# A hybrid decoder trunk on one core: side tasks of the first mixer handed out per row tile and held between projection matmuls, the residual's transposes held until the output projection

## The chip, the cores and the metric

The kernel runs on one core of one Trainium2 chip. The time is the device time of one execution in microseconds (us). The kernel before was timed three times on the chip, and once more under the hardware profiler; all numbers of the trace below come from that profiled execution.

## What is computed

A trunk of two residual layers over 256 tokens of width 2048, in float32. Each layer is a mixer, a cross-attention into 256 memory tokens, and a SwiGLU feed-forward block; each of the three normalises its input and adds its result to the residual stream `h`.

```
for layer in range(2):
    hn = rms_norm(h, ln_mix[layer])
    mix = nsa_retention_mixer(hn, ...) if layer == 0 else gated_deltanet_mixer(hn, ...)
    h = h + mix
    h = h + memory_cross_attention(rms_norm(h, ln_mem[layer]), mem, ...)
    h = h + swiglu_ffn(rms_norm(h, ln_ffn[layer]), ...)
```

The first mixer has one input projection. It feeds eight attention heads (a branch over compressed blocks, one over selected blocks, one over a window; at 256 tokens all blocks are selected) and four retention heads. The compressed branch takes overlapping blocks of 32 tokens and sends them through a small two-layer network (`nsa_cmp_w1`, `nsa_cmp_w2`). An output projection joins all heads.

## The kernel before, in words

**Projections.** Activations lie transposed in SBUF, 128 features to a tile. A projection (`Proj`) loops over the 16 row tiles of its weight (44 in the output projection of a feed-forward block). `load_weight` fetches 512 KB by DMA from the queue of SyncE (SP), two row tiles of 512 columns at a time, into four buffers. `split_weight` (L214, L215) splits each piece of 128 x 512 into a high part, rounded to fp32r by ScalarE (ACT), and the low rest, by VectorE (DVE); four buffers hold each. `passes` (L237) then issues three fp32r matmuls per product: high by high, high by low, low by high. In the form "f" (weights stationary) a row tile of 512 columns is four column blocks of three passes, 12 matmuls with 256 moving columns. In the form "t" (activations stationary) it is two token halves of three passes, 6 matmuls with 512 moving columns. The four column blocks write two PSUM tiles, two blocks in each.

**Work beside projections.** Everything else is written as generators, called tasks: they do a piece of work and yield a number. `Proj.step` counts issued work in units of a 256-column matmul; each time 6 units are full, `tick` advances a counter `now` by one and resumes each task that is due. A task that yields n is due 2n counts later, at least 1. A row tile is 12 units, so before the change there are two ticks in a row tile, and `yield 1` is one row tile. `finish(ts)` ticks on the spot, with no projection between, until the given tasks are done. Four PSUM banks serve the tasks; `take(n)` waits for n of them, `give(n)` returns them.

**Order on the engines.** The program is traced in the order above. A scheduler then orders each engine's queue by a timeline of its own: an instruction traced earlier goes first if its data are there by then, and a later one passes it if they are not. `tc.issue_after(i)` adds an order edge: what is traced inside the block on the engine of `i` stands behind `i` in that engine's queue. On the chip each queue runs in its order.

**The first mixer** (`mix0`, L699). `nsa_keys` projects keys and values in three projections of 16 row tiles, then spawns the two tasks `compress`, one for keys and one for values. Two query projections of 16 row tiles follow; behind each, four heads of the generator `head` are spawned. `finish(cmp)` ends the compress tasks. `retention` follows with eight projections of 16 row tiles, in two groups (query, key, value, gate); at the end of each group two tasks `ret_head` are spawned, and those of the first group are finished on the spot. The output projection is `residual` with `early=12`: the first 12 row tiles of two of its four column groups go first.

`compress` (L858 on) loads `nsa_cmp_w1` in 8 loads of 512 KB, each for four steps of k, and yields 1 after every second k: 16 yields, 4 matmuls before each (L882, L883; the shape is 128 x 256). Its tail follows: copy (L887), transposes (L890), sigmoid, second product (L901 or L912), norm, and the copy of the keys to `kcat` (L908).

`head` waits until both compress tasks are done and takes three banks. It issues the scores (L795 to L798) and two transposes for the queries' norm (L386); a chain over ACT and DVE turns them into scaled softmax rows `s` (L801 to L828); `yield 5`; it transposes `s` (L833 to L838) and copies the results to SBUF (`pTc` L839, `px` L842, `py` L843); `yield 2`; it multiplies with the values (L847 to L851), and gives its banks back. `ret_head` issues scores, `yield 2`, products, `yield 3`, transposes (L986).

**The last feed-forward block** (`ffn`, L626 on). 11 pairs of projections (gate and up, form "f") fill the hidden activations; 4 output projections in the form "t" follow, 44 row tiles each. Beside the first of these the task `turn` transposes the residual stream back: 8 groups of 4 transposes (L672), each copied by ACT (L675) with `yield 2` after it.

Of the kernel before, what the change touches and what calls it, by code (L numbers as in the profile page):

```python
# [2 lines left out]

# [1 line left out]

# [13 lines left out]
P = 128  # L19
# [59 lines left out]
def trunk(ctx: ExitStack, tc: tile.TileContext, a: dict, out: bass.AP, phases=ALL):  # L79
# [7 lines left out]
    sp = ctx.enter_context(tc.tile_pool(name="sp", bufs=2))  # L87

    sp.tile([P, 112], F32, name="pad", bufs=1)
    state = {"now": 0, "banks": 4, "wide": None}  # L90
    dp = ctx.enter_context(tc.tile_pool(name="dp", bufs=1, space=DRAM))
    psj = ctx.enter_context(tc.tile_pool(name="psj", bufs=4, space=PSUM))
    psg = ctx.enter_context(tc.tile_pool(name="psg", bufs=4, space=PSUM))
# [18 lines left out]
    def tick():  # L112
        state["now"] += 1
        for t in list(tasks):
            if t.ready <= state["now"]:
                try:
                    t.ready = state["now"] + max(1, int(2 * (next(t.gen) or 1)))
                except StopIteration:
                    t.done = True
                    tasks.remove(t)  # L120
# [97 lines left out]
    def load_weight(W, k0, nk, c0, ncol, g=None):  # L218
# [10 lines left out]
            parts += [(h[:, i, :], l[:, i, :]) for i in range(m)]  # L229
        return parts  # L230

    def passes(o, x, w, start, last, x_stationary=False):

        (xh, xl), (h, l) = x, w
        pairs = ((xh, h), (xh, l), (xl, h)) if x_stationary else ((h, xh), (h, xl), (l, xh))
        for j, (s_, m) in enumerate(pairs):
            PE.matmul(o, s_, m, start=start and j == 0, stop=last and j == 2, skip_group_check=True)  # L237

    class Proj:

# [50 lines left out]

        def step(self, n):
            self.count += n
            while self.count >= 6:
                self.count -= 6
                tick()

    def proj(W, c0, segs, x, KT=KD, g=None):
        return Proj(W, c0, segs, x, KT, g).run()
# [254 lines left out]
    def cross_attention(l, side):  # L554
        with pool("xax", side=side) as xx, pool("xas") as xs, pool("xa", 2) as xp:
            xb = split_x(xx)
            x = fill_x(xb, 1, l)
            kt = xs.tile([P, 4, T], F32, name="kt")
            vt = xs.tile([P, 2, 512], F32, name="vt")
            S.dma_start(kt, kv[l][0])  # L560
# [65 lines left out]
    def ffn(l, last):  # L626
        Wi, Wo = a["ffn_w_in"][l], a["ffn_w_out"][l]
        with pool("ff") as fp, pool("ft", 2) as ft:
            hh = fp.tile([P, KF, T], F32R, name="hh")
            hl = fp.tile([P, KF, T], F32R, name="hl")  # L630
            with pool("ffx", side="right") as fx:
                x = fill_x(split_x(fx), 2, l)
                rb = None
                ns = None
                for b in range(KF // 4):
                    pg = proj(Wi, b * 512, [("f", 512)], x)[0]
                    if rb is None:
                        rb = rstd_bc()
                    gs = []
                    for i in range(2):  # L640
                        g = ft.tile([P, 2, T], F32, tag="fg", name="fg", bufs=3)
                        for j in range(2):
                            V.tensor_mul(g[:, j], pg[i][:, j], rb)
                        ns = S.activation(g, g, AF.Silu)
                        gs.append(g)
                    pu = proj(Wi, FH + b * 512, [("f", 512)], x)[0]
                    for i in range(2):
                        g = gs[i]
                        k = 4 * b + 2 * i
                        u = ft.tile([P, 2, T], F32, tag="fu", name="fu")  # L650
                        for j in range(2):
                            V.tensor_mul(u[:, j], pu[i][:, j], rb)
                        V.tensor_mul(u, u, g)
                        S.activation(hh[:, k : k + 2], u, AF.Copy)
                        V.tensor_sub(hl[:, k : k + 2], u, hh.bitcast(F32)[:, k : k + 2])
                with tc.issue_after(ns.ins):
                    S.preload_act_table_set(LNEXP)
            hx = lambda k: (hh[:, k, :], hl[:, k, :])
            if not last:
                residual(Wo, hx, KF)  # L660
                return
            with pool("ffo", side="right") as fo:

                xt = fo.tile([P, 2, D], F32, name="xt")

                def turn():
                    for b in range(4):
                        for t in range(2):
                            yield from take(1)
                            p = bank()  # L670
                            for f in range(4):
                                PE.transpose(  # L672
                                    p[:, f * P : (f + 1) * P], xT[:, b * 4 + f, t * P : (t + 1) * P], ident
                                )
                            S.activation(xt[:, t, b * 512 : (b + 1) * 512], p, AF.Copy)  # L675
                            give(1)
                            yield 2

                spawn(turn())
                for b in range(4):  # L680
                    po = proj(Wo, b * 512, [("t", 512)], hx, KF)[0]
                    for t in range(2):
                        o = xt[:, t, b * 512 : (b + 1) * 512]
                        V.tensor_add(o, o, po[t])
                        S.dma_start(out[0, t * P : (t + 1) * P, b * 512 : (b + 1) * 512], o)
# [13 lines left out]
    def mix0(xb, close):  # L699
        W = a["hyb_w_in"][0]  # L700
        done = {}
        with pool("m0o") as op:
            oh = op.tile([P, 16, T], F32R, name="moh")
            ol = op.tile([P, 16, T], F32R, name="mol")
            cm = op.tile([P, 512 + 4 * 384 + 1], F32, name="cmix")
            S.dma_start(cm, a["c_mix"])
            with pool("ns") as np_:
                x = parts(xb)
                ck = pool("cmpk", side="right")
                with pool("wide", 2) as state["wide"]:  # L710
                    nsa, cmp = nsa_keys(W, x, np_, ck.__enter__(), cm)
                with pool("nt", 2) as nt:
                    for blk in range(2):
                        pq = proj(W, blk * 512, [("f", 512)], x)[0]
                        for i in range(4):
                            h = blk * 4 + i
                            q = nt.tile([P, T], F32, tag="q", name="q", bufs=8)
                            S.activation(q, pq[i // 2][:, i % 2, :], AF.Copy)
                            done[h] = spawn(nsa(nt, h, q, oh, ol))
                    finish(cmp)  # L720
                    ck.__exit__(None, None, None)
                    with pool("rt", 2) as rt_:
                        retention(W, x, rt_, oh, ol, cm, done)

                        def mo(k):
                            finish([done[k]])
                            return oh[:, k, :], ol[:, k, :]

                        residual(a["hyb_w_out"][0], mo, 16, early=12)
                        drain()  # L730
            close()
# [263 lines left out]

    def mix1():
        W = a["gdn_w_in"][0]
        with pool("gr") as r_:


# [533 lines left out]
```

## Time and profile before

| | us |
|---|---|
| median of 3 runs | 3003.91 |
| lowest, highest | 3001.68, 3008.66 |
| the profiled execution, its own time | 3001.64 |
| its span, first to last instruction | 2999.8 |
| TensorE (PE) busy in the span | 2957.6 |
| VectorE (DVE) busy | 2033.3 |
| ScalarE (ACT) busy | 1703.5 |

The mean granted TensorE clock is 0.997 of its upper level, 2.4 GHz. Matmuls overlap in the array, so a matmul's own duration (about 280 ns for 256 columns) is longer than the time from its start to the next one's. The pace of a stream is therefore its time divided by its matmuls. A float32 matmul of the tasks that is not a transpose stands in the trace as two records.

### The profile page before, as it was taken

To read this page: it belongs to the slowest core of one execution; us is meant where nothing else is said; L and a number is where in the kernel's file an instruction comes from. 1 tells how busy PE (TensorE), PEld (TensorE's weight loads), DVE (VectorE), ACT (ScalarE), POOL (GpSimd) and SP (SyncE) were. 2 spreads that over 40 slices of the span, in tenths; PEclk is the share of its full clock that TensorE was granted. 3 is DMA by queue.
4 is the path that set the end of the run, shared out by engine and by line. 5 is a ranking of instruction groups with operands and counts; after the bars stand their busy time and mean duration, and the time that the engine had idled before them with its cause. 6 is when DMAs were issued, how large, how long until landed. Compare 5 with 4: busy or idle time off the path is not lost.

```text
span 2999.8 us, 59557 instructions
## 1 busy us (share of the span) xinstructions
PE 2957.6 (99%) x22917; PEld 2830.7 (94%) x22917; DVE 2033.3 (68%) x3879; ACT 1703.5 (57%) x3328; POOL 110.3 (4%) x153
## 2 busy tenths in 40 slices
PE   8999999999999999999999989999999999999999
PEld 8989899999999999999978989999999999999887
DVE  6867676776665665557689978886667656655554
ACT  6655655665555554447665657776556555445444
POOL 0000000000000000000110101121000000000000
PEclk9999999999999999999999999999999999999999
DMA  7776555656666665566677676663656666666665
GB/s 237 203 233 178 156 147 176 186 174 195 193 195 193 195 195 193 196 191 187 185 220 230 178 208 178 176 177 127 194 187 182 191 193 194 184 189 183 197 199 166
DMA packets 327641, 566.97 MB, mean 189 GB/s; under 512 B 41868, under 2 KB 71620, under 8 KB 327100
## 3 DMA queue, kind: packets, MB, share of 16 engines
q1 hardware_dynamic: 321280, 545.02, 61.0%
q10 hardware_dynamic: 3500, 10.33, 1.3%
q0 software_dynamic: 2576, 7.82, 0.9%
q8 instruction: 179, 2.93, 0.4%
q14 instruction: 106, 0.87, 0.1%
HBM read 549.16 MB, written 13.93 MB: 188 GB/s over the span
## 4 chain that ended last, share of the span: by engine, by line
PE 94%; DMA 2%; DVE 2%; ACT 1%; issue 1%; POOL 0%; SPq 0%; ACTq 0%; DVEq 0%; POOLq 0%
PE pj L237 87%; DVE w_lo L215 1%; DMA w<-in_hyb_w_in 1%; DMA d_T<-AB 1%; PE slv L1458 0%; PE slv L1455 0%; PE slv L1444 0%; ACT w_hi L214 0%; DMA w<-in_nsa_cmp_w 0%; DVE xT L424 0%; POOL AB L1350 0%; DVE x_lo L357 0%; DMA mraw<-in_mem 0%; PE slv L1452 0%; PE qk L1071 0%
## 5 line engine op out<-in xcount | busy, mean ns | idle before, releaser
L215 DVE TENSOR_TENSOR w_lo<-w,w_hi 128x512 fp32r<-128x512 f32 x1938 | 1328.0, 691 | 829.9 <-ACT w_hi L214 818.2
L214 ACT ACTIVATE w_hi<-w 128x512 fp32r<-128x512 f32 x1938 | 1215.1, 631 | 1127.5 <-DVE w_lo L215 591.8
L237 PE MATMUL pj<-x_hi,w_hi 128*128 128x256 f32 (+1 forms) x4496 | 1248.4, 280 | 16.0 <-ACT w_hi L214 15.7
L237 PE MATMUL pj<-x_lo,w_hi 128*128 128x256 f32 x4496 | 1244.0, 279 | 0.0
L237 PE MATMUL pj<-x_hi,w_lo 128*128 128x256 f32 (+1 forms) x4496 | 1225.2, 280 | 0.9 <-DVE w_lo L215 0.9
L237 PEld LDWEIGHTS pj<-x_hi,w_hi 128*128 128x128 f32 (+1 forms) x4496 | 848.4, 189 | 19.5 <-ACT w_hi L214 17.4
L237 PEld LDWEIGHTS pj<-x_lo,w_hi 128*128 128x128 f32 x4496 | 845.6, 188 | 0.8
L237 PEld LDWEIGHTS pj<-x_hi,w_lo 128*128 128x128 f32 (+1 forms) x4496 | 831.6, 188 | 3.2 <-DVE w_lo L215 2.3
L237 PE MATMUL pj<-hl,w_hi 128*128 128x256 f32 x704 | 193.7, 276 | 0.0
L237 PE MATMUL pj<-hh,w_hi 128*128 128x256 f32 x704 | 193.6, 276 | 0.0
L237 PE MATMUL pj<-hh,w_lo 128*128 128x256 f32 x704 | 192.4, 276 | 0.0
L237 PE MATMUL pj<-o,w_hi 128*128 128x256 f32 x1024 | 182.4, 281 | 1.3 <-ACT o L1013 1.1
L237 PE MATMUL pj<-w_lo,x_hi 128*128 128x512 f32 (+2 forms) x448 | 172.0, 385 | 2.6 <-DVE w_lo L215 2.3
L237 PE MATMUL pj<-w_hi,x_lo 128*128 128x512 f32 (+2 forms) x448 | 168.0, 376 | 0.0
L237 PEld LDWEIGHTS pj<-o,w_hi 128*128 128x128 f32 x1024 | 155.9, 189 | 2.0 <-ACT o L1013 1.3
L237 PE MATMUL pj<-o,w_lo 128*128 128x256 f32 x512 | 141.6, 281 | 0.0
L237 PE MATMUL pj<-w_hi,x_hi 128*128 128x512 f32 (+2 forms) x448 | 140.5, 380 | 0.5 <-ACT w_hi L214 0.4
L237 PE MATMUL pj<-w_hi,hl 128*128 128x512 f32 x352 | 138.3, 393 | 0.0
L237 PE MATMUL pj<-w_lo,hh 128*128 128x512 f32 x352 | 137.7, 391 | 0.0
L237 PEld LDWEIGHTS pj<-hh,w_hi 128*128 128x128 f32 x704 | 132.1, 188 | 0.0
L237 PEld LDWEIGHTS pj<-hl,w_hi 128*128 128x128 f32 x704 | 132.1, 188 | 0.0
L237 PEld LDWEIGHTS pj<-hh,w_lo 128*128 128x128 f32 x704 | 131.3, 188 | 0.0
(416 smaller groups left out, 3613.1 us busy)
## 6 DMA issues: line engine op xcount, KB each, us to landing
w<-in_ffn_w_in SPq DMA_DIRECT2D x352, 512.0 KB, 4.2
w<-in_gdn_w_in SPq DMA_DIRECT2D x193, 512.0 KB, 4.2
w<-in_ffn_w_out SPq DMA_DIRECT2D x176, 512.0 KB, 3.7
w<-in_hyb_w_in SPq DMA_DIRECT2D x96, 512.0 KB, 3.7
w<-in_gdn_w_out SPq DMA_DIRECT2D x64, 512.0 KB, 4.4
w<-in_xa_wkv SPq DMA_DIRECT2D x32, 512.0 KB, 4.4
w<-in_hyb_w_out SPq DMA_DIRECT2D x32, 512.0 KB, 4.7
w<-in_nsa_cmp_w SPq DMA_DIRECT2D x16, 512.0 KB, 5.0
```

Source lines behind the costliest of these rows:

```text
L214: state["hi"] = S.activation(h, w, AF.Copy)
L215: state["lo"] = V.tensor_sub(l, w, h.bitcast(F32))
L237: PE.matmul(o, s_, m, start=start and j == 0, stop=last and j == 2, skip_group_check=True)
```

## The change

In the first mixer `state["beat"]` is 12 instead of 6, until the cross-attention sets it back. A tick then comes once in a full row tile; `now` still advances by two in it. A task sleeps at least 4 counts, two row tiles. The tick runs inside `together`: all matmuls and transposes that the tasks trace in it stand behind the last projection matmul traced, and the next projection matmul stands behind the last of them in trace order. Ticks of `finish` are not held. In the last feed-forward block the transposes of `turn` stand behind the last projection matmul traced when they are traced; its beat stays 6.

```diff
-    state = {"now": 0, "banks": 4, "wide": None}
+    state = {"beat": 6, "now": 0, "banks": 4, "wide": None}
...
-                    t.ready = state["now"] + max(1, int(2 * (next(t.gen) or 1)))
+                    t.ready = state["now"] + max(4 if state["beat"] > 6 else 1, int(2 * (next(t.gen) or 1)))
...
+    @contextmanager
+    def together():
+
+        traced = nc.cur_bb.bb.instructions
+        n = len(traced)
+        mm = state["mm"].ins
+        with tc.issue_after(mm):
+            yield
+        own = [i for i in traced[n:] if i.engine == mm.engine]
+        if own:
+            state["after"] = own[-1]
+
     def passes(o, x, w, start, last, x_stationary=False):
...
         for j, (s_, m) in enumerate(pairs):
-            PE.matmul(o, s_, m, start=start and j == 0, stop=last and j == 2, skip_group_check=True)
+            after = state.pop("after", None)
+            with tc.issue_after(after) if after is not None else nullcontext():
+                state["mm"] = PE.matmul(o, s_, m, start=start and j == 0, stop=last and j == 2, skip_group_check=True)
...
         def step(self, n):
             self.count += n
-            while self.count >= 6:
-                self.count -= 6
-                tick()
+            while self.count >= state["beat"]:
+                self.count -= state["beat"]
+                state["now"] += state["beat"] // 6 - 1
+                if state["beat"] > 6:
+                    with together():
+                        tick()
+                else:
+                    tick()
...
             x = fill_x(xb, 1, l)
+            state["beat"] = 6
...
-                            for f in range(4):
-                                PE.transpose(
-                                    p[:, f * P : (f + 1) * P], xT[:, b * 4 + f, t * P : (t + 1) * P], ident
-                                )
+                            with tc.issue_after(state["mm"].ins):
+                                for f in range(4):
+                                    PE.transpose(
+                                        p[:, f * P : (f + 1) * P], xT[:, b * 4 + f, t * P : (t + 1) * P], ident
+                                    )
...
     def mix0(xb, close):
         W = a["hyb_w_in"][0]
         done = {}
+        state["beat"] = 12
...
     def mix1():
         W = a["gdn_w_in"][0]
+        state["beat"] = 6
```

## Rows read from the trace of the kernel before

**Rows 1.** The page: busy times of the engines; shares of the chain that ended last.
```profile
PE 2957.6 (99%) x22917; PEld 2830.7 (94%) x22917; DVE 2033.3 (68%) x3879; ACT 1703.5 (57%) x3328; POOL 110.3 (4%) x153
...
PE 94%; DMA 2%; DVE 2%; ACT 1%; issue 1%; POOL 0%; SPq 0%; ACTq 0%; DVEq 0%; POOLq 0%
```

**Rows 2.** Stretches: length, busy PE PEld DVE ACT POOL (x), granted clock, DMA share, GB/s.
```profile
188.00:231.00 43.00, 39.27 (x317) 37.72 (x316) 33.91 (x60) 28.98 (x58) 0.00 (x0) 1.00 0.90 276
231.00:262.60 31.60, 31.49 (x255) 29.64 (x255) 20.57 (x58) 18.55 (x53) 0.00 (x0) 1.00 0.63 188
262.60:371.00 108.40, 108.40 (x703) 97.86 (x701) 78.10 (x224) 62.40 (x166) 0.00 (x0) 1.00 0.54 155
```

**Rows 3.** The chain that ended last, in pieces: start, us, what, matmuls merged.
```profile
269.34 0.43 PE nC L847 x2
...
494.56 88.34 PE pj L237 x750
...
653.36 706.41 PE pj L237 x6188
...
2488.03 0.33 PE g L672 x3
2488.36 43.54 PE pj L237 x384
...
2532.01 224.69 PE pj L237 x1888
```

**Rows 4.** The residual's transposes: all of them, and the one at 2531.74 us.
```profile
L672 PE MATMUL g<-ident,xT x32: 270/272/273, 2312.4 to 2764.6; 128*128 128x128 f32 x32
...
2531.74 0.27 PE L672 MATMUL g<-ident,xT 128*128 128x128 f32 x1
```

**Rows 5.** PE by line, 188 to 262.6 us: count, busy us, mean ns, idle before.
```profile
L237 PE MATMUL pj<-x_hi,w_hi 128*128 128x256 f32 x133 | 36.8, 284 | 0.5 <-ACT w_hi L214 0.5
...
L882 PE MATMUL cmp<-w_hi,cfp 128*128 128x256 f32 x64 | 16.5, 290 | 3.2 <-ACT w_hi L214 3.2
```

**Rows 6.** ACT in order of time: start of the copies behind the second query projection.
```profile
262.62 0.62 ACT L718 ACTIVATE q<-pj 128x256 f32<-128x256 f32 x2
```

**Rows 7.** DMA from 188 to 231 us: packets, and compress's loads.
```profile
DMA packets 9864, 11.88 MB, mean 276 GB/s; under 512 B 366, under 2 KB 7805, under 8 KB 9860
...
w<-in_nsa_cmp_w SPq DMA_DIRECT2D x14, 512.0 KB, 5.0
```

**Rows 8.** One head in order of time on PE and DVE: start us, us, engine, line.
```profile
272.28 0.38 PE L386 MATMUL nC<-ident,q 128*128 128x128 f32 x2
...
282.81 0.75 DVE L828 TENSOR_SCALAR s<-s,st 128x16 f32<-128x16 f32 x3
...
283.96 0.27 PE L838 MATMUL nB<-ident,s 128*7 128x128 f32 x1
...
292.66 0.39 PE L851 MATMUL nC<-py,vw 128*128 128x128 f32 x2
...
293.32 0.38 PE L386 MATMUL nC<-ident,q 128*128 128x128 f32 x2
```

**Rows 9.** The tail of compress in order of time: its first and its last instruction.
```profile
233.42 0.37 ACT L887 ACTIVATE chs<-cmp 60x256 f32<-60x256 f32 x1
...
249.21 0.24 DVE L908 COPY kcat<-kn 128x15 f32<-128x15 f32 x2
```

**Rows 10.** Busy time by stretch, columns as in rows 2: two standstills of PE.
```profile
149.50:153.00 3.50, 0.67 (x6) 0.46 (x4) 0.33 (x1) 0.99 (x2) 0.00 (x0) 1.00 0.97 278
...
1780.00:1782.00 2.00, 0.00 (x0) 0.00 (x0) 0.00 (x0) 0.00 (x0) 0.00 (x0) 1.00 0.64 157
...
1784.00:1786.00 2.00, 0.00 (x0) 0.00 (x0) 0.00 (x0) 1.29 (x6) 1.26 (x2) 0.50 1.01 388
```

**Rows 11.** PE in order of time: the output projection's first matmul, the retention heads' last transposes.
```profile
482.18 0.28 PE L237 MATMUL pj<-moh,w_hi 128*128 128x256 f32 x1
...
494.18 0.38 PE L986 MATMUL rs<-ident,ry 128*128 128x128 f32 x2
```

More of the change, by code (lines that the diff above doesn't have):

```diff
@@ L1 @@
 import math
-from contextlib import ExitStack
+from contextlib import ExitStack, contextmanager, nullcontext
 import numpy as np
```

## The prediction

> **What bounds the kernel now.** I read the page first: TensorE is busy for 99% of the span and holds 94% of the chain that ended last, the vector engine is at 68% [rows 1]. So a change pays only where the matmul queue stands still or runs below its best pace, and it costs where it makes that queue wait. The change touches two stages: the first mixer (from about 114 to 583 us) and the last feed-forward block (2267 to 2998 us). I then read the stages by stretches [rows 2]: in the mixer PE has idle time in one stretch only, 188 to 231 us, where the two compress tasks load their weights beside the first query projection and DMA runs at 276 GB/s; from 262.6 us on PE is busy without a break. "Busy" hides the pace, so the third view is the chain in pieces, as time per matmul [rows 3]. A piece of 384 projection matmuls takes 43.54 us, 113.4 ns each, and the 6188 of the first feed-forward block 114.2 ns (a few wide ones among them). But 750 in a row from 494.56 us, most of them the first mixer's output projection, take 88.34 us, 117.8 ns each, with nothing between them. There are two paces, 4.4 ns apart, and a stream keeps the one that it has until something else is put into it. The last feed-forward block shows the moment of a fall: at 2531.74 us one hoisted transpose of the residual stands between two passes of one product, and the 1888 matmuls behind it take 224.69 us, where the five like pieces before it ran at 113.4 ns [rows 3, 4].
>
> **The transposes of the last block.** All 32 transposes of `turn` are traced beside the output projection, yet run from 2312.4 us on [rows 4], up to 440 us early, at several places three together. Three cost 0.33 us on the chain and will cost it at their new place, so 32 are 3.5 us before and after. What goes is the slow pace behind the last hoisted one: 1888 x (117.8 - 113.4) ns = 8.3 us. By the piece itself it would be 224.69 - 1888 x 0.1134 = 10.6 us, but its end holds the first wider matmuls of the output projection, so 10.6 is the upper end. The lower end is zero, if some other event sets the slow pace. I take 8.3: after the change nothing is left to interrupt that stream, and the same stream in the first block kept the fast pace for 706.41 us [rows 3]. The output stage needs the transposed residual only when a whole projection of 44 row tiles is done (about 60 us), so eight groups, two row tiles apart, are hidden there; no DMA and no queue but PE, and ACT's eight copies behind it, sees them move.
>
> **The first mixer: compress.** A row tile is 12 matmuls, 1.36 us. Work beside it was handed out twice per row tile; it is now handed out once, and a task sleeps at least two row tiles. The compress loop, 16 steps of one row tile each, so stretches from 16 to 32 row tiles, the whole of both query projections. Its 16 loads of 512 KB leave SP's queue in the order of the handing out, so they are spread too, between the projections' 16. Now: from 188.0 us to the copies of the second query block at 262.62 [rows 6], 74.6 us pass. PE issued in them some 400 projection matmuls (three groups of about 133, one of them shown) and 2 x 64 of compress [rows 5], 528 x 0.1134 = 59.9 us; of the 572 matmuls in all [rows 2] 44 are others, 5.9 us at an estimated 0.13, a little over a transpose's 0.11: 65.8 us. So 8.8 us are lost, 3.7 of them as idle time before 231 us [rows 2]. After: 32 loads are 16.8 MB, 61 us at the 276 GB/s that DMA gave [rows 7], less than PE's 66. PE sets the time, with little to spare. Gain between 0 (DMA no better placed) and 8.8; I take 7, as most of the demand that overran DMA is moved to where DMA now runs at 188 GB/s [rows 2].
>
> **The first mixer: the hold.** Each tick's matmuls now stand behind the last projection matmul traced, and the first pass of the next row tile stands behind the last of them. If one waits for its data, that pass waits too, and with it everything that accumulates into its bank. What may go on are the other three column blocks of the next rows, as far as four split weights reach: 4 rows x 9 passes = 36 matmuls, 4.1 us. Today the scheduler simply lets a late task slide: the head that I followed has its scores at 272.28 us, its scaled scores finished at 283.56, its first transpose at 283.96 and its output at 292.66 [rows 8], and the next head's scores end 21 us after its own, though the yields ask for 7 row tiles.
> The first head is held worst. Compress now ends at row tile 31 of 32, so its tail (copy, transposes, sigmoid, second product, norm) runs after the second query projection, and the head's scores behind that. The transposes are due five row tiles later. Data: tail 16.1 us now, 233.42 to 249.45 [rows 9], of which its bare instructions are some 8.5; scores 1.8; scores to scaled scores 272.66 to 283.56, 10.9 [rows 8]; together 21 to 29 us. PE has six row tiles (8.2), tail and scores (3.3) and the 4.1 that may run ahead: 15.6. PE stands for 5 to 13 us. Elsewhere a standstill from 1780 us on brought the granted clock from 1.00 to 0.50 by 1784, while one inside 149.5 to 153 us left it at 1.00 [rows 10]; some 6 us of work at half clock would cost 3 us more. I take 6: the tail is long now because its matmuls stand behind projection matmuls that will be used up.
> The seven other heads come every 8 row tiles: PE has 8 x 1.36 + 4.4 for the head = 15.3 us of work (a 256-wide float32 product is 0.43 [rows 3], the others in proportion: scores 1.8, transposes 0.9, output 1.7); a head's own cycle is 1.8 + 10.9 + last transposes and copies 1.2 + output 1.7 + 0.5 to the next = 16.1. So 0.8 us each, 5.6 us; between 0 and 7 x (10.9 - 5 x 1.36) = 29, if nothing may run ahead. I take 4, as the vector engine is freer of split weights while PE waits. The retention heads of group 0 are handed out without a hold. Those of group 1 are held at the start of the output projection; now their last transposes come 12 us after its first matmul, 482.18 to 494.18 [rows 11], and the hold gives them six row tiles (8.2), their own products (5) and the 4.1: nothing.
> Last, the output projection behind the mixer, and the first of the next stage, run at the slow pace now: 750 x 4.4 ns = 3.3 us. Which pace it has after the change depends on the last held group; I count half, 1.6.
>
> **Sum.** -8.3 - 7 + 6 + 4 - 1.6 = -6.9 us against the profiled execution's own 3001.6 us (span 2999.8): 2994.7. The median of the runs shown, 3003.9, is 2.3 us above that execution, so 2997.0. A change under 0.2%, 6 us, can hardly be told from none here.
>
> **Rivals.**
> (a) The mixer gains all it can: the holds cost nothing because their data are there, compress gives 8.8 and the output projection is fast. -8.3 - 8.8 - 3.3 = -20.4: 2983.5. For it: PE is the only full engine. Against it: the cycle of 16.1 against 15.3.
> (b) The pace is not what the transpose set, or the transposes in the output stage only trade one slow stretch for another; the mixer is even. Then the time is that of before, 3004. Against it: five pieces of 384 before 2531 us and the whole first block are fast. The Trainium skill, "TensorE: Matmul & The Clock Gate", section "Back-to-back issue gap", gives one gap for a width, N/2.4 + 2.5 ns, an estimated 109 ns here, and knows no second pace. By that rule the holds buy nothing; the two rows at 113.4 and 117.8 with clock and width the same speak against it. An equal result comes if the mixer costs 8 where I have 1.4.
> (c) Slower: the hold turns the heads' latency into PE time. Place: the transposes of each head, 5 row tiles behind its scores. If nothing runs ahead of a held pass, each waits 10.9 - 6.8 = 4.1 us, 7 x 4.1 = 29 us, and the first head 9 more: -8.3 - 7 + 29 + 9 - 1.6 = +21: 3025. It decides from about 1.6 us per head on, where the sum turns positive. For it: a head takes 21 us now and is asked for in 15.3; the rotary work of two projections stands in the vector engine's queue as well. Against it: the scheduler reorders passes of different column blocks already.
>
> **Chances.** Forecast (2991 to 3000) 0.46, (a) 0.14, (b) and an even sum 0.20, (c) in any size above +6 us 0.20. The forecast's larger part, below 2998, and (a) with its near cases make faster 0.48; (b) and the rest of the forecast same 0.31; slower 0.21. For 8 in 10 the range reaches to (a)'s end, 2984, and to half of (c), 3014.
>
> **What will show it.** Right: no transposes of the residual before 2750 us, and the gate and up projections at 113.4 ns to their end; compress over some 60 us without DMA waits; the heads every 15 to 17 us. Wrong: PE idle before a head's transposes in more than the first head, a granted clock below 1.00 in the mixer, or a stretch of 117.8 ns in the last block all the same.

## The result, and the profile after

The changed kernel takes 3024.13 us (median of 4 runs, 3021.59 to 3026.58), the kernel before 3002.8 in the runs beside it: a ratio of 1.0065, 95% interval 1.0053 to 1.0077. It is slower by some 0.65%; the forecast of 2997 and its range up to 3014 are both missed. The profiled execution took 3021.59 us, its span is 3019.8 against 2999.8.

The page of the changed kernel, busy times and shares of the chain that ended last:

```profile
PE 2961.8 (98%) x22917; PEld 2827.4 (94%) x22917; DVE 2038.7 (68%) x3879; ACT 1709.8 (57%) x3328; POOL 111.5 (4%) x153
...
PE 92%; DVE 3%; DMA 2%; ACT 1%; issue 1%; POOL 0%; ACTq 0%; SPq 0%; DVEq 0%; POOLq 0%
```

Against [rows 1] the instructions are as many, PE is busy 4.2 us longer and the span is 20 us longer. Most of the time was not worked, it was waited.

To find where, the mixer is cut at copies that both kernels make. A begins at the copy of the last key and value projection and ends at the copies of the second query projection (compress runs here). B goes on to the first gate copy of retention group 0, four projections later (the heads run here). C ends at the first value copy of group 1. The stretches A, B and C of the changed kernel (length; busy PE, PEld, DVE, ACT, POOL; granted clock; DMA share, GB/s):

```profile
191.03:258.00 66.97, 65.91 (x509) 61.66 (x510) 46.25 (x77) 42.12 (x80) 0.00 (x0) 1.00 0.81 243
258.00:409.33 151.33, 133.88 (x805) 115.76 (x804) 100.75 (x328) 78.92 (x243) 0.00 (x0) 0.95 0.40 113
...
409.33:485.57 76.24, 76.20 (x534) 71.04 (x533) 52.41 (x106) 39.31 (x73) 0.00 (x0) 1.00 0.59 170
```

The same stretches A, B and C of the kernel before:

```profile
190.08:262.62 72.54, 68.70 (x554) 65.31 (x553) 52.49 (x114) 46.02 (x107) 0.00 (x0) 1.00 0.79 241
262.62:370.38 107.76, 107.76 (x698) 97.29 (x697) 77.48 (x221) 61.78 (x166) 0.00 (x0) 1.00 0.55 156
370.38:457.32 86.94, 86.94 (x608) 80.54 (x607) 65.52 (x177) 48.87 (x123) 0.00 (x0) 1.00 0.51 146
```

There B and C have no idle time, at a clock of 1.00. B has grown by 43.6 us, and stands idle for 151.33 - 133.88 = 17.5 of them; C is 10.7 shorter, since heads that slid into C before are done in B. A is 5.6 shorter. With 0.9 us lost ahead of A, 2.6 less in the gate projection behind C, 2.7 more in the output projection, which now has the retention heads' rest in it, and 1.1 less in the stage after it, the mixer is 27.2 us behind. Another 1.2 us is lost on the way to the last block, and there 8.4 are won: 20.0.

PE's waits from 258 to 410 us (waiting tile, for whom: us in all, times, longest):

```profile
PE nB L860 <- DVE s L850: 10.3, 4, 6.3
PE nA L855 <- DVE s L850: 6.2, 7, 1.3
PE nA L818 <- DVE kcat L930: 0.8, 1, 0.8
```

L855 and L860 are the heads' transposes, `s` their scaled scores: 16.5 of the 17.5 us are PE standing in front of a transpose whose data are not there. One head, in order of time (in brackets the wait ahead of an instruction):

```profile
305.84 0.38 PE L405 MATMUL nC<-ident,q 128*128 128x128 f32 x2
...
318.32 0.62 DVE L850 TENSOR_SCALAR s<-s,st 128x7 f32<-128x7 f32 x3
...
318.61 0.28 PE L860 MATMUL nB<-ident,s 128*7 128x128 f32 x1 [1.83 <-DVE s L850]
...
319.60 0.75 DVE L850 TENSOR_SCALAR s<-s,st 128x16 f32<-128x16 f32 x3
...
320.14 0.33 PE L855 MATMUL nA<-ident,s 128*128 128x128 f32 x1 [0.82 <-DVE s L850]
```

Compare [rows 8]. Between the last scores and the first transposes of the seven later heads the trace has 72 to 84 projection matmuls (counted as 256 wide), where the kernel before let some 92 to 97 pass in most heads; the first head has none there. The chain over DVE and ACT is not shorter for that: here 305.84 to 320.35 us. PE stands twice, because the scores of the second token half are ready 1.4 us after those of the first. And the standstills have a second price. Three short stretches behind them (columns as above):

```profile
280.00:287.00 7.00, 5.59 (x24) 4.95 (x25) 3.51 (x14) 3.46 (x10) 0.00 (x0) 0.54 0.00 0
...
316.00:324.00 8.00, 5.35 (x29) 4.62 (x28) 4.08 (x17) 4.36 (x16) 0.00 (x0) 0.79 0.17 60
...
357.00:361.50 4.50, 3.68 (x13) 2.88 (x13) 1.66 (x7) 1.61 (x3) 0.00 (x0) 0.62 0.00 0
```

The clock fell from its upper level to the lower one. Up to 7 x 0.46 + 8 x 0.21 + 4.5 x 0.38 = 6.6 us of work are lost so, beside the idle time; a part of it falls into idle time and is counted twice.

What the forecast had right stands in the pieces of the chain, and in the transposes of the residual by line:

```profile
525.47 85.37 PE pj L251 x753
...
2313.25 457.66 PE pj L251 x4035
2770.91 0.44 PE g L693 x4
...
L693 PE MATMUL g<-ident,xT x32: 271/272/273, 2770.8 to 2793.7; 128*128 128x128 f32 x32
```

The gate and up projections run in one piece at 113.4 ns a matmul, and the transposes wait until the output projection [rows 3, 4]. The first mixer's output projection is at 113.4 ns too, where it was at 117.8.

### The profile page after: what moved, and what is told of

It reads as the page before. It is cut to its first block, busy times and chain, and to the rows that moved or that the text cites. A ratio compares the mean times of both kernels' runs of the same rounds, so it can differ in the third digit from the quotient of the medians.

```text
span 3019.8 us, 59529 instructions
## 1 busy us (share of the span) xinstructions
PE 2961.8 (98%) x22917; PEld 2827.4 (94%) x22917; DVE 2038.7 (68%) x3879; ACT 1709.8 (57%) x3328; POOL 111.5 (4%) x153
## 4 chain that ended last, share of the span: by engine, by line
PE 92%; DVE 3%; DMA 2%; ACT 1%; issue 1%; POOL 0%; ACTq 0%; SPq 0%; DVEq 0%; POOLq 0%
PE pj L251 85%; DVE w_lo L215 1%; DMA d_T<-AB 1%; ACT w_hi L214 0%; PE slv L1481 0%; PE slv L1478 0%; DMA w<-in_hyb_w_in 0%; PE slv L1467 0%; DVE xT L443 0%; PE cmp L905 0%; ACT s L846 0%; POOL AB L1373 0%; DVE x_lo L376 0%; DMA mraw<-in_mem 0%; PE slv L1475 0%
```

## The experiments

Theory H: the hold itself costs, as PE waits for the heads' chain. Theory B: the rarer and later handing out costs. In the expectations a stage's loss is its length less its matmuls at the fast pace (113.2 ns for a projection's of 256 columns, about 2 ns and 0.83 ns a column for one record of a float32 one). Lengths and losses, in us, with the ratio to before and its interval; worked out from the time lines of the profiled runs (one execution each):

```
                           A           B           C       ratio
before                  72.5  9.7  107.8  1.6   86.9  1.4  1
changed kernel          67.0  9.0  151.3 30.9   76.2  2.1  1.0065 [1.0053, 1.0077]
e1  transposes only     73.0 10.8  107.8  1.6   86.9  1.4  0.9972 [0.9962, 0.9982]
e2  no hold             59.8  2.6  109.8  2.7  102.1 12.7  0.9980 [0.9970, 0.9990]
e3  heads free          67.9  9.9  107.8  3.0  106.2 16.4  1.0020 [1.0012, 1.0029]
e4  only heads held     59.4  2.2  145.2 24.8   77.5  1.3  1.0019 [1.0008, 1.0029]
e5  e4, sleep 7         60.7  3.5  129.5 14.0   82.9  1.8  0.9986 [0.9977, 0.9995]
e6  all held, sleep 7   67.2  9.3  133.8 16.9   79.7  2.0  1.0033 [1.0024, 1.0043]
e7  edge in front only  67.6 10.3  107.8  3.0  107.2 17.4  1.0035 [1.0022, 1.0048]
e9  e5, first head 11   59.7  2.0  121.7 11.8   89.0  2.1  0.9978 [0.9968, 0.9988]
e10 e5, first head free 60.5  3.3  130.6 15.0   83.0  1.8  1.0001 [0.9992, 1.0010]
e11 edge behind only    60.6  2.8  149.9 29.9   79.0  2.3  1.0050 [1.0037, 1.0063]
e13 e1, compress 24     64.1  6.2  109.4  1.2   96.3  8.8  0.9978 [0.9967, 0.9988]
e14 e1, compress 20     70.4 10.3  109.2  1.3   92.8  6.5  0.9979 [0.9970, 0.9989]
```

Two things have to be kept in mind with these rows. Runs with the same mixer as e1 (e8, e12, e15 to e18; e17 differs only behind C) have an A of 71.1 to 74.0 us, so 1 or 2 us in A are nothing; their B and C agree to 0.1. And the output projection behind C, which no column holds, ran at the fast pace in the changed kernel, e3 to e7, e9 to e11, e13 and e14, and at the slow pace in the kernel before, e1 and e2: 3 us.

**e1: the last block's transposes alone.**

```diff
     def mix0(xb, close):
...
-        state["beat"] = 12
+        state["beat"] = 6
```

> The mixer stays as before (two ticks in a row tile, no hold); only the 32 transposes of the last block are held until the output projection. Both theories on the mixer expect the same here: all 4035 matmuls of the last gate and up stream at 113.4 ns, 8.3 us less than before, about 2994.5. If that stream's pace hung on something else in the changed kernel, a stretch of 117.8 ns stays in the last block and the time is 3003.

Measured 0.9972, 8.4 us of 3005.7. The piece of the chain:

```profile
2289.19 457.67 PE pj L251 x4035
```

As expected to 0.1 us. The same kernel on another chip (e18) gave 0.9970.

**e2: no hold in the mixer.**

```diff
-                if state["beat"] > 6:
-                    with together():
-                        tick()
-                else:
-                    tick()
+                tick()
```

> The changed kernel without the hold in the mixer: one tick in a row tile, sleeps of at least two row tiles, but the tasks' matmuls may slide. Theory H (the hold makes PE wait for the heads' vector and scalar chain): the heads' idle time before their transposes and the falls of the granted clock go, 25 to 30 us less than the changed kernel, 2992 to 2998. Theory B (handing out late is the fault: compress ends behind the second query projection, the heads start late and bunched): at most 8 us less than the changed kernel, above 3015, with the idle time between 258 and 410 us still over 8 us.

Measured 0.998, 2998.1 us: H's side. But the table shows something that neither theory had. A loses 2.6 us instead of 10.8: the stretched compress does save what the forecast claimed. B is even. C loses 12.7. PE's long wait there, and the two ends of the heads' stretch (the keys' copy that lets the first head begin; the first scores of a retention head, which here wait for `mol`, the last instruction of an attention head):

```profile
PE nB L856 <- DVE s L846: 5.2, 1, 5.2
```
```profile
261.79 0.23 DVE L926 COPY kcat<-kn 128x15 f32<-128x15 f32 x2
...
420.97 0.48 PE L979 MATMUL rs<-rqk 128*128 128x256 f32 x1 [0.28 <-DVE mol L871]
```

That is 159.2 us. In the kernel before it is 249.21 [rows 9] to 409.35, 160.1; in e1 160.1, in e3 158.9, in e7 159.6. In these versions eight unheld heads take some 160 us whenever they begin. PE is nearly full in that time (idle for 1.4 us of it in e2, 3.6 in e3), so it is not shown what sets the 160 us, the heads' own chain or the projection matmuls that pass them. PE has projections to run meanwhile only for a time: the first copy of a group 1 projection to `rqk`, which the retention heads of group 0 still read, comes 0.8 us after the start of their last scores in both kernels (426.74 after 425.95 before, 435.14 after 434.35 in e2); there is one buffer for it. Before, PE's projections and the heads ended together. In e2 the heads begin 12.6 us later, and the last one has no projection matmul left between its last scores and its first transposes, where before it had 97. With unheld heads, whoever makes A shorter, or the heads later, makes PE wait in C.

**e3 and e4: who is held.** Tasks get a mark; a tick holds each task by itself, in e3 all but the eight heads, in e4 only them.

```diff
-                    t.ready = ... next(t.gen) ...
+                    with together() if hold and not t.free else nullcontext():
+                        n = next(t.gen)
```

> The changed kernel with the hold kept for every task but the eight attention heads, whose matmuls may slide. Theory H: as without any hold within 4 us, 2992 to 2999, the granted clock at 1.00 between 262 and 430 us. Theory B: above 3015. A third way, the hold costs at compress and retention as well: in between, 3002 to 3015.

> The mirror of the run before: only the eight heads are held, compress, the key norms and the retention heads may slide. Theory H: within 4 us of the changed kernel, 3020 to 3028, with PE's idle time before the heads' transposes over 10 us. Theory B: the same time too, so this run only tells whether the hold of the other tasks adds or gives something: compress free could gain the 1 to 4 us that its hold costs between 162 and 258 us.

Measured 1.0020 and 1.0019: e3 came by the third way that its text named, and for e4 both theories were wrong. Each half of the hold costs by itself. Held heads: B loses 24.8, and the heads' stretch shrinks to 129 us (262.13 to 391.17), so C loses nothing. Held compress: A loses 9.9 against 2.6. What ACT's splits wait for in A, in e2 and then in e3:

```profile
ACT w_hi L214 <- PE pj L251: 5.0, 9, 0.9
```
```profile
ACT w_hi L216 <- PE pj L253: 17.5, 19, 1.4
```

With the hold the splits wait three and a half times as long for projection matmuls to give up their split pieces: 17.2 us in the changed kernel, too. (In the kernel before, without a hold but with compress in 16 row tiles, it is 14.4 us, so the wait is no sign of the hold alone.) PE itself shows hardly any idle time in A for it, as a halt shorter than a matmul's own duration does not show. By the time lines, in the changed kernel 44 steps from one matmul to the next are 0.1 to 0.25 us longer than at the fast pace, 6.2 us in all; in e2 it is 10 steps and 1.2 us.

**e7 and e11: one edge of the hold at a time.** e7 lets the next projection matmul pass the tasks' last; e11 lets the tasks' matmuls go ahead of the projection matmul before them.

```diff
# e7
-            state["after"] = own[-1]
+            pass
# e11
-        with tc.issue_after(mm):
-            yield
+        yield
```

> The changed kernel with one of the two order edges of the hold: the tasks' matmuls still stand behind the last projection matmul traced, but the next projection matmul need not stand behind them. If the cost is that the projection waits for the tasks (theory H), the time is that of the run without a hold within 4 us, 2995 to 3002. If the cost lies in the tasks' not being allowed earlier (rival), it is near the changed kernel, 3018 to 3027.

> The changed kernel with the other one of the two edges: the next projection matmul stands behind the tick's last task matmul, but the tasks' matmuls may go earlier than the projection matmul before them. From the two runs with one and no edge: the heads' loss comes from this edge, so the stage behind the second query projection loses 25 to 31 us as in the changed kernel; compress's loss came from the other edge (10 us with it, 2.6 without), so between 190 and 258 us 2 to 4 us are lost: 5 to 7 us less than the changed kernel, 1.004 to 1.005 of before. If either edge alone costs compress its gain, 1.006 to 1.007.

e7 took 3017.5 us, 1.0035: between the two times that its text named, and nearer the rival's. The stages separate it. Held back only from going early, compress loses 10.3, the heads next to nothing in B, and C pays 17.4 for heads that begin late. e11 came as expected: 2.8 in A, 29.9 in B. So the edge in front costs compress its gain, and the edge behind turns the heads' latency into PE time. The splits' wait for the projection in A, in e7 and then in e11:

```profile
ACT w_hi L214 <- PE pj L251: 19.4, 19, 1.5
```
```profile
ACT w_hi L214 <- PE pj L250: 4.6, 11, 0.8
```

**e5 and e6: a longer sleep before the transposes**, in e4 and in the changed kernel.

```diff
-            yield 5
+            yield 7
```

> As the run in which only the eight heads are held, but a head sleeps 7 row tiles instead of 5 between its scores and its transposes. Theory H (a held transpose turns what its head's vector and scalar chain of some 11 us is late into PE time): two row tiles more are 2.7 us more cover per head, so the idle time before the transposes falls below 5 us in all, the granted clock stays at 1.00 behind the first head, the loss of that stage falls from 25 us to 5 to 8, and since compress is free (2 us lost instead of 10) the time is 2988 to 2996. Theory S (each hold stops the stream by itself, whatever the sleep): within 5 us of the run with 5, 3005 to 3013. Third way: with ten row tiles to a head the last two heads are handed out at the end of the first retention group, and PE stands there as without any hold: some 10 us more, 2998 to 3006.

> The changed kernel with 7 row tiles instead of 5 between a head's scores and its transposes, every task held. Theory H: 18 to 24 us less than the changed kernel, 1.0065 of before, so 0.9985 to 1.0005 of before, about 3001 to 3007; compress still loses 9 to 10 us under its hold. Theory S: no more than 5 us less than the changed kernel, over 1.005.

Two row tiles more took 10.8 us off B in e5 and 14.0 in e6, so the latency is the cause and not the hold's mere presence; S falls. The size was overrated: the 18 to 24 us of e6 came as 10. What stays in e5 is mostly the first head (of its waits in B):

```profile
PE nB L858 <- DVE s L848: 4.9, 2, 4.4
PE nA L853 <- DVE s L848: 2.5, 4, 0.7
```

**e9 and e10: the first head**, which sleeps 11 row tiles (e9) or is free (e10), on top of e5.

```diff
# e9
-            yield 7
+            yield 11 if h == 0 else 7
# e10
-                            done[h] = spawn(nsa(nt, h, q, oh, ol))
+                            done[h] = spawn(nsa(nt, h, q, oh, ol), h == 0)
```

> Only the eight heads are held, with 7 row tiles between a head's scores and its transposes, and 11 for the first head, whose scores come behind the tail of compress. Theory H: the 4.6 us before the first head's transposes and the fall of the granted clock behind them go, the stage from the second query projection's end to the first group's value projection loses 3 to 5 us instead of 12.8; against before 0.9950 to 0.9965. If the first head's standstill is only moved to the next head, 0.998 to 1.000.

> As the run before, but the first head is not held at all and sleeps 7 like the others; heads two to eight are held. Theory H: the same 0.9950 to 0.9965, if the first head slides by no more than the two row tiles of slack that a later head has; if its sliding makes the second head's scores late, the second head's transposes stand 3 to 5 us, and 0.997 to 0.9985.

Both missed. e9: 0.9978, B loses 11.8. The first head's 4.4 us are 1.0, but the other heads now wait instead; e10 is no better than before. The waits of e9 in B, and a stretch behind its first head:

```profile
PE nB L858 <- DVE s L848: 2.7, 3, 1.3
PE nA L853 <- DVE s L848: 2.3, 3, 0.8
```
```profile
275.00:300.00 25.00, 23.75 (x172) 0.93 0.39 108
```

Behind two waits of 1.0 and 0.8 us, at the first head, the clock fell; behind two of 1.3 and 0.8 us at the fourth head of the same run it did not (granted clock 1.00 from 330 to 345 us). A held head needs slack for its slowest chain, and the chains differ by 4 us.

**e13 and e14: compress over 24 and 20 row tiles**, on top of e1.

```diff
                 if k % 2:
-                    yield 1
+                    yield 1.5                            # e13
+                    yield 1.5 if k % 4 == 3 else 1       # e14
```

> The transposes of the last block held, the mixer without any hold and with two ticks in a row tile as before; only compress sleeps 1.5 row tiles instead of 1 between its steps, 24 row tiles in all instead of 16. The term of the prediction for compress (stretching it saves 7 of the some 10 us lost between 190 and 263 us) holds if it is the crowding that costs: half way in row tiles, 3 to 7 us less than with the transposes alone, 0.9950 to 0.9965 of before. If the heads' later start is given back at the end of the first retention group, as in the run without a hold, 1 to 6 us of it come back there as idle time, 0.9965 to 0.998.

> As the run before, with compress over 20 row tiles (sleeps of 1 and 1.5 in turn). If crowding costs and falls evenly with the stretch: 2 to 4 us less than with the transposes alone, 0.996 to 0.997 of before, and nothing comes back at the end of the first retention group, as the heads start only four row tiles later.

Nothing is won at the end: 0.9978 and 0.9979 against e1's 0.9972, though both had their output projection at the fast pace and e1 had not. In e13 A loses 4.6 us less and C 7.4 more; in e14 A gains next to nothing and C still loses 5.1 more. Their heads' stretch is even 164 and 168 us. A saving ahead of the heads is a saving only if they end earlier with it.

**e8, e12, e15, e16: what sets the pace.** All four stand on top of e1. e8 holds seven of the eight groups of the residual's transposes. The others hold all of them and add four, two or three transposes of it, into a tile that nothing reads, between the second and the third pair of gate and up projections.

```diff
# e8
-                            with tc.issue_after(state["mm"].ins):
+                            with tc.issue_after(state["mm"].ins) if (b, t) != (0, 0) else nullcontext():
# e12 (e15: range(2), e16: range(3))
+                xt4 = fx.tile([P, 512], F32, name="xt4")
...
+                    if last and b == 2:
+                        pt_ = bank()
+                        with together():
+                            for f in range(4):
+                                PE.transpose(pt_[:, f * P : (f + 1) * P], xT[:, f, 0:P], ident)
+                        S.activation(xt4, pt_, AF.Copy)
```

> The mixer as before; of the eight groups of four transposes of the residual, seven are held and the first may run early, into the gate and up stream. Theory P (a stream keeps the pace that the last interruption gave it): everything behind the last of these four, up to 4000 matmuls, runs at one pace until the output projection: either 113.4 ns, then the time is that of the run with all held, 0.997 of before, or 117.8 ns, then 1890 to 3750 matmuls cost 8 to 16 us, 1.000 to 1.0025 of before. Rival (the slow pace comes from many transposes, or from the output stage): 113.4 ns within 50 us behind the four wherever they stand, and 0.997 of before; a mean between the two paces over hundreds of matmuls would speak against both.

> The run with all of the last block's transposes held, and four transposes more (of the residual, into a tile that nothing reads), held together between the second and the third pair of gate and up projections: 0.45 us by themselves. If it is a single transpose that leaves the slow pace behind it, and a group the fast one (three left it fast, one left it slow), all stays at 113.4 ns and the time is 0.997 to 0.9978 of before. If any interruption may leave either pace by the moment at which the stream restarts, the 3450 matmuls behind the four run at 117.8 ns with some chance, 15 us more, 1.001 to 1.003.

> As the run with four transposes more between the second and third pair of gate and up projections, with two in place of four. If the number of interposed transposes decides the pace (three left it fast, one and four slow), it has one definite pace for all 3450 matmuls behind: by a rule of threes 117.8 ns, 1.001 to 1.003 of before; by odd and even, which one and three already break, no forecast. If each restart is a chance, either pace.

> The control: three transposes at the same place. If the number decides, all 3450 matmuls behind them stay at 113.4 ns, as behind the threes of the kernel before: 0.997 to 0.9978 of before. If it is the order edges of the added group, or its place, that leave the slow pace, 117.8 ns and 1.001 to 1.003.

Pieces of the chain of e8, and of e12, e15 and e16:

```profile
2313.68 0.33 PE g L693 x3
2314.01 43.53 PE pj L251 x384
2357.54 0.11 PE g L693
2357.65 404.66 PE pj L251 x3420
```
```profile
2351.83 0.44 PE g L661 x4
2352.27 407.74 PE pj L251 x3459
```
```profile
2354.21 0.22 PE g L661 x2
2354.43 392.38 PE pj L251 x3459
```
```profile
2351.41 0.33 PE g L661 x3
2351.73 392.38 PE pj L251 x3459
```

One transpose, 0.11 us, leaves 3420 matmuls at 118.3 ns with a few wide ones among them; e8 is 1.0019 [1.0010, 1.0028] and so 14 us behind e1. Four leave 117.9 (e12 1.0032 [1.0019, 1.0045]), three 113.4 (e16 0.9959 [0.9947, 0.9971]). Two can leave either: the profiled execution of e15 has 113.4 ns, and its 12 times fall into two groups, 2996.0 and 2997.5, and ten from 3007.4 on (1.0014 [1.0000, 1.0028]). The ten were not traced; that they had the slow pace is inferred from their times. The stretches of e12 and e16 behind the transposes, columns as in [rows 2]:

```profile
2352.27:2760.01 407.74, 407.74 (x3461) 407.56 (x3461) 240.94 (x398) 202.88 (x327) 0.00 (x0) 1.00 0.65 187
```
```profile
2351.73:2744.11 392.38, 392.38 (x3462) 392.21 (x3461) 241.14 (x398) 202.59 (x327) 0.00 (x0) 1.00 0.61 194
```

PE is busy throughout both, at the same granted clock. So theory P holds, the last restart sets the pace for thousands of matmuls; by the times of e15, one and the same program, the number alone does not decide it, and what does stays open.

**e17: the second group's retention heads held**, on top of e1, beside e1 again (e18).

```diff
+        with together() if h > 1 else nullcontext():
             for t in range(2):
                 for c in range(2):
                     PE.transpose(b[:, ...], ys[t][:, ...], ident)
```

> The transposes of the last block held, the mixer without a hold, and the last transposes of the two retention heads of the second group held (behind the last projection matmul traced, the next one behind them). In the four runs so far in which those were held the output projection behind them lost 0.4 to 0.8 us, with the slow pace 3.1 us. If the hold settles the pace there, 2.5 us less than with the last block's transposes alone, 0.9958 to 0.997 of before, and 113.4 ns behind the last of those transposes. If the pace is a matter of chance at each restart, 117.8 ns is as likely, and the time is that of the last block's transposes alone, 0.997.

> The kernel of the first run again, beside the run above on the same chip: only the last block's transposes held. 0.9962 to 0.9982 of before as then; its output projection at 117.8 ns, 2.5 us behind the run above if the hold settles the pace.

0.9976 [0.9965, 0.9987] and 0.9970 [0.9958, 0.9981]: no gain, and the output projection of e17 is at 117.8 ns. In ten of the other runs that stage was fast, some with those heads held and some without. Holding does not choose the pace. Nor does it look like chance in this place: in all the runs with the mixer of e1, and in the kernel before, it was slow.

No version beat e1 with an interval clear of e1's own (e16, which does the same and three transposes more, comes nearest with 0.9959 [0.9947, 0.9971]); e1 is 8.4 us faster than the kernel before and some 28 us faster than the changed one.

## Why the prediction was wrong, point by point

**The transposes of the last block, -8.3: right.** 8.4 in the trace, 8.4 in e1 by itself, with the step that it named: the last interruption goes, the pace stays. Rival (b) is out: e12 and e16, which differ by one transpose, have 117.9 and 113.4 ns for the same 3459 matmuls. The Trainium skill ("TensorE: Matmul & The Clock Gate", section "Back-to-back issue gap") gives the formula N/2.4 + 2.5 ns for an isolated matmul; of a stream of weight loads and matmuls it says that both set the spacing, and it names no second pace for one width. The trace differs: it is a stream of that second kind (as many weight loads as matmuls, [rows 1]) and has both paces, 113.4 and 117.9 ns.

**Compress, -7: right without the hold, wrong with it.** The sum behind it is a little off (44 others at 0.13 us are 5.7 us and not 5.9, so 9.0 are lost and not 8.8), and PE is idle elsewhere in the mixer too (4.4 us from 113 to 190 us, [rows 10] among them); neither bears on the result. e2 loses 2.6 us in that stage instead of 10.8. The changed kernel loses 9.0. The step that failed: the hold was costed for the heads only, and compress was treated as if its matmuls could still go when their weights came. The edge in front alone takes the gain back (e7 against e11). And even unheld the 7 us would not have shown in the total: the argument held PE to be the one full engine, and did not see that from the keys' copy to the first retention head the unheld heads take just as long beside it: some 160 us (e2, e3, e7), 164 and 168 in e13 and e14. Held heads take 129 to 141, so the 160 is no fixed length of their chains; it belongs to the order in which the unheld ones slide.

**The first head, +6: right in place, and in size for the idle time.** The waits at its transposes are 6.3 and 0.8 us, and the clock stays at the lower level behind it, some 3.2 us by the stretch from 280 us. The text had that as a possible 3 more and left it out: about 10 in all.

**The seven other heads, +4: the step that failed most.** They cost some 19 us, 2.7 a head where the prediction had 0.6: B's loss of 30.9, less the 1.6 that it had before and the 10.3 of the first head (waits of 6.3 and 0.8, and 3.2 by the clock). Two numbers in it were wrong. First, 36 matmuls were allowed to run ahead of a held pass; the trace has 72 to 84 between scores and transposes, the 60 of five row tiles and 12 to 24 more. Second, the head followed in [rows 8] was one of the shortest: from scores to scaled scores it took 10.9 us, but the seven later heads of the kernel before have a mean of 11.7 and one of 14.4, where the rotary work of a projection falls between, and in the changed kernel they have 10.8 to 14.2, mean 12.1. With 12.1 against 78 matmuls, 8.8 us, an estimate gives 3.3 us a head, twice the 1.6 from which rival (c) was said to decide. The measured waits ahead of their transposes are less, 9.4 us in all or 1.3 a head, in part since the first transposes need only the first token half, some 1.4 us earlier; the clock behind two of these heads costs up to 3.4 more, and the rest of the 19 is not resolved. The trace of the kernel before had the longer chains.

**The output projection's pace, -1.6: it came whole,** 117.8 to 113.4 ns over 753 matmuls, 3.3 us. Counting half was right in kind: e17 shows that it is no matter of the hold.

**Rival (c)** had the place, the mechanism and, at 3025, the time. Its sum was right by luck, by two errors that cancel: heads and first head at 38 us instead of about 29, and compress at -7 instead of about 0. Of its two signs both came: idle time ahead of most heads' transposes, and a granted clock below 1.00 in the mixer.

What was not tried: more buffers for the split pieces or for the second group's keys, which would tell whether compress could stay held, and the heads late, at no cost.

## What to carry to other kernels

An order edge in a full queue is free only where the data are surely there: cost it with the longest of the chains that it waits for, not with the one followed, and for each task that it covers, not only for the slow one. An engine at 99% can have a row of tasks beside it that takes just as long, and then work saved ahead of these tasks comes back behind them as a wait; look for the two events that bracket them and see from version to version whether their distance changes. Let nothing small run in a long uniform stream if it can wait until the stream's end.

## What the runs showed of the hardware

A stream of fp32r matmuls with 256 columns has two paces at the same granted clock, 113.4 and 117.8 ns, and keeps for over 400 us the one at which it restarted. Three interposed transposes left it fast each time (five times in the kernel before, in e8 and, by its five times, in e16), one and four slow, two, by the times of e15, now the one and now the other from execution to execution of one program: some 10 us of difference with nothing changed. A comparison of two kernels within 0.4% can be this and nothing else. The clock fell to its lower level behind standstills of 1.83 and 0.82 us in one head, with PE busy before and between, while [rows 10] had one of 2.8 us in 3.5 without a fall. What the length of a standstill does to it, these runs do not settle.
